# Moving weights read from two runs of 256 columns in turn, in a one-core decoder layer on Trainium2

## The chip, the cores and the metric

The kernel runs on one core of a Trainium2 chip. The metric is the device time of one execution in microseconds, lower is better. Three runs of the kernel before took 429.0, 428.86 and 430.1 us, median 429.0.

The core has five engines that matter here: TensorE (PE in the profile; its weight loads are listed apart as PEld), VectorE (DVE), ScalarE (ACT), GpSimd (POOL) and SyncE (SP), which here only issues DMA transfers. A matmul has a stationary operand, 128 columns that are loaded into the array first, and a moving operand, whose columns are then read one by one. Its result goes to a bank of PSUM, 128 partitions by 512 numbers of 32 bits.

## The reference

One layer of a decoder over 256 tokens of width 1024. Three attention mixers read one combined projection of x; their outputs go through branch projections and gates and are added. What matters for this change is what follows:

```
merged = (gates[:, :, 0] * (o_a @ w_br_a[i])
          + gates[:, :, 1] * (o_b @ w_br_b[i])
          + gates[:, :, 2] * (o_c @ w_br_c[i]))
x = layer_norm(ALPHA * x + merged @ w_out[i], ln1_g[i], ln1_b[i])
h = jnp.square(jax.nn.relu(x @ w_up[i])) @ w_down[i]
ple = jax.nn.sigmoid(x @ w_ple_gate[i]) * (p[i] @ w_ple[i])
x = layer_norm(ALPHA * x + h + ple, ln2_g[i], ln2_b[i])
```

`w_out` and `w_ple_gate` are 1024 x 1024, `w_ple` is 256 x 1024, `w_up` 1024 x 4096 and `w_down` 4096 x 1024, all in 32-bit floats.

## The kernel before

**Products in three terms.** Every operand is split into a high and a low part in the 32-bit format that PE multiplies in one pass. `prod` (L184, its matmul on L189) adds high x high, high x low and low x high into one bank of PSUM. So each product of a stationary block and a moving block is three matmuls, and each of these has its own weight load.

**The weights.** `Weights` (L80) holds a list of units. For each, SP issues one transfer of up to 128 x 1024 numbers from HBM into a ring of five buffers (`raw`, L103); ScalarE writes the high part (`whi`, L110 or L112); VectorE, for some units with GpSimd, subtracts it to make the low part (`wlo`, L119 or L123). `get` does this up to four units ahead of the use. The order of the work on each engine is written by a planner that estimates times; `pin` keeps single instructions in program order.

**Two kinds of product.** In the gates, the branch projections and the up projection the weights are the stationary operand, in blocks of 128 columns, and the activations move. There the code spreads the blocks in `whi` and `wlo` with gaps (`LOW`, L223; `UP`, L606). In the output projection, the embedding, its gate and the down projection it is the other way round: the activations are stationary, 128 tokens at a time, and the weights move, 512 columns at a time (`H` are the two halves of the 1024 columns). These blocks stand in `whi` and `wlo` without gaps.

**The stages with moving weights, in order:**

- *Output projection:* class `Wide` (L611) over the 8 blocks of 128 rows of `w_out`. For each block, two halves of the tokens (b) and two halves of the columns (c): 8 x 4 products. `go` (L623) makes one.
- *Embedding:* 2 blocks of rows of `w_ple` (`wp`, L753), 4 products each, scaled into `PL`.
- *Its gate:* `Wide` again over the 8 blocks of `w_ple_gate`; the stationary blocks are the normalised x, transposed (`x1`). The first normalisation (`ln1`) runs between.
- *Up projection:* 32 blocks, stationary weights, L891 (512 columns) and L893 (256 columns). Not of the moving kind. `relu2` and the split write the hidden activations `hT`.
- *Down projection:* `SEQ` (L819) lists the 26 blocks of its loop. Seven pairs of blocks are done by a scheme of Strassen's kind: `form` (L848) makes sums and differences of the halves of two blocks' weights, and seven products in place of eight go to seven banks (`TERMS`, `onto`, L932). Twelve single blocks go through `plain` (L944), 4 products each. Then the banks are added up, and the 6 blocks of `LATE` (L821) are added per output bank, with the second normalisation (`ln2`, L992) behind each. For the last quarter of the tokens and columns the last 512 columns are cut into two of 256 (`CUT`, L983), so that their normalisation can start earlier.

**What depends on the columns' order.** The split works column by column. `form` adds and subtracts whole halves of 512. The normalisations, the sums over banks and the output read PSUM in the natural order of columns.

**The host** (`_layout`, L1064) only reorders: it reshapes `w_out`, `w_down`, `w_ple_gate` and `w_ple` into blocks of 128 rows with all 1024 columns in their own order.

Of the kernel before, what the change touches and what calls it, by code (L numbers as in the profile page):

```python
# [19 lines left out]
D = 1024  # L20
# [123 lines left out]
def hybrid_layer(ctx: ExitStack, tc: tile.TileContext, x0, xn, pT, wqk, wva, wvb, wg, wbc, wba,  # L144
# [26 lines left out]
    ph = keep.tile([128, 2, S], F32R, name="ph")  # L171
    pl = keep.tile([128, 2, S], F32R, name="pl")
# [5 lines left out]
    t = banks.tile([128, 512], F32, name="b4", tag="b4")  # L178
# [5 lines left out]
    def prod(ps, a, b, first, last, hold=False, more=False, low=2):  # L184

        terms = [(0, 0), (0, 1)]
        terms.insert(low, (1, 0))
        for n, (x, y) in enumerate(terms):
            i = pe.matmul(ps, lhsT=a[x], rhs=b[y], start=first and n == 0, stop=last and n == 2,  # L189
                          skip_group_check=more)  # L190
            if hold and n == 0:
                pin(i)

    def gemm(ps, units, xs, k=0):

        for u in units:
            hi, lo = W.get(u)
            for o in range(0, hi.shape[1], 128):
                prod(ps, (hi[:, o:o + 128], lo[:, o:o + 128]), xs[k], k == 0, k == len(xs) - 1,
                     low=TURN["g"][k])  # L200
                k += 1
# [29 lines left out]
    for t in TASKS:  # L231
# [4 lines left out]
        elif t in "gcao":  # L236
            u, w, n = {"g": (u_g, wg, 1024), "c": (u_bc, wbc, 640), "a": (u_ba, wba, 768),
                       "o": (u_out, wout, 1024)}[t]
# [28 lines left out]
    def mmbank(shape):  # L267
        t = mm.tile([128, 512], F32, name="mm", tag="mm")
        return t[:, 0:256] if shape == 256 else t

    last = [None, None]
# [20 lines left out]
    def k_pair(a, b=None):  # L292


        k = (kp if b is None else k1).tile([128, 2, S], F32R, name="k", tag="k")
        for d, ps in ((slice(0, 128), a),) if b is None else ((slice(0, 64), a),
                                                             (slice(64, 128), b)):
            freed(act.copy(k[d, 0], ps),
                  dve.tensor_tensor(k[d, 1], ps, k[d, 0].bitcast(F32), op=ALU.subtract))  # L299
        return k  # L300
# [28 lines left out]
    def feat(f):  # L329
        ps = mmbank(256)  # L330
        gemm(ps, u_q[f], xs)
        if f > 8:
            next(side, None)
        return ps
# [133 lines left out]
    with ExitStack() as begin:  # L468
# [7 lines left out]
        with tc.high_priority(offset=1000):  # L476
# [4 lines left out]
            for k in range(KT):  # L481
                act.copy(xh[:, k], g0[:, k, 0:S])
                for a, b in cut[k]:
                    a = max(a, S)
# [3 lines left out]
        first = [next(ps_s if f < 3 else ps_t)[:, 0:S] for f in range(FIRST)]  # L488
# [8 lines left out]
    ps = feat(4)  # L497
# [35 lines left out]
    def opair():  # L533
        return wk2.tile([128, S], F32, name="o", tag="o")

    for j in range(2):
        ps = feat(5 + 4 * j)
        k = k_pair(ps)
# [6 lines left out]
        o = opair()  # L545
# [11 lines left out]
    for j in range(3):  # L557
        ps = feat(13 + 2 * j)
        k = k_pair(ps)
        q = q_pair(feat(14 + 2 * j))  # L560
        s = logits(k, q)
        o = opair()
# [12 lines left out]
    for j in range(3):  # L575
        s = logits(kA, q)
        o = opair()
# [31 lines left out]
    H = (slice(0, 512), slice(512, 1024))  # L609

    class Wide:  # L611
# [10 lines left out]

        def go(self, acc, k, b, cs, first, last, hold=False, more=False):  # L623
            hi, lo = self.ws[k]
            prod(acc, self.stat(k, b), (hi[:, cs], lo[:, cs]), k == first, k == last, hold, more)

        def step(self, k, ahead=AHEAD, bs=(0, 1), last=None, whole=None):

# [54 lines left out]
    more = p3.tile([128, 4096], F32R, name="more")  # L683
# [54 lines left out]
    def turn(b, c, ps):  # L738

        pt[b, c] = ps = ps.rearrange("p (k t) -> p k t", t=128)  # L740
        for k in range(4):
            pin(pe.transpose(ps[:, k], Y[:, b, (4 * c + k) * 128:(4 * c + k + 1) * 128], ident))  # L742
        return act.copy(x1[:, b, 4 * c:4 * c + 4, 0], ps)
# [9 lines left out]
    wp = [W.get(u, 0) for u in u_ple]  # L753
    for i in range(4):
        if i == 3:
            turn(0, 0, next(ps_a))
            low(0, 0)
        b, cs = i // 2, H[i % 2]
        t = slice(b * 128, (b + 1) * 128)
        ps = mmbank(512)  # L760
        for k in range(2):
            prod(ps, (ph[:, k, t], pl[:, k, t]), (wp[k][0][:, cs], wp[k][1][:, cs]),
                 k == 0, k == 1, True)
        act.mul(PL[:, b, cs], ps, 0.5)

# [57 lines left out]
    hT, at, room = {}, 0, 0  # L823
    for k in (*SEQ, *LATE):
        i = PAIRS.index(k) if k in PAIRS else -1
        n = 512 if i < 0 else 1792
        if i in (0, 1):
            t = p2.tile([128, 2048], F32R, name=("X", "PL")[i], tag=("X", "PL")[i])[:, 0:n]
        elif i in (2, 3) or k == 2:
            t = more[:, room:room + n]  # L830
            room += n
        else:
            t = store[:, at:at + n]
# [31 lines left out]
    for k in (*SEQ, *LATE):  # L865
        if k in PAIRS:
            i = PAIRS.index(k)
# [13 lines left out]
    for f in range(32):  # L881
# [5 lines left out]
        ps = mmbank(512).rearrange("p (b a t) -> p b a t", b=2, a=2)  # L887
        hi, lo = W.get(u_up[f][0])
        cs = [slice(k * 128, (k + 1) * 128) for k in range(KT)]
# [26 lines left out]
        h = hT[half_of[f]]  # L916
# [11 lines left out]
    P = {2: pg.acc[1][0], 3: pg.acc[1][1], 4: pg.acc[0][0], 8: pg.acc[0][1], 7: next(ps_a)}  # L928
    P.update((i, mmbank(512)) for i in (5, 1, 6))
    fresh = {1, 5, 6, 7}  # L930

    def onto(i, a, b, end=False):  # L932
        prod(P[i], a, b, i in fresh, end, more=True)
        fresh.discard(i)

    def weights(u):
# [7 lines left out]
    def plain(k, w, ids, end=False):  # L944
        for i in ids:
            b, c = {2: (1, 0), 3: (1, 1), 4: (0, 0), 8: (0, 1)}[i]
            t, cs = slice(128 * b, 128 * b + 128), H[c]
            onto(i, (hT[k][:, 0, t], hT[k][:, 1, t]), (w[0][:, cs], w[1][:, cs]), end)


    TERMS = ((2, 2, 1), (3, 6, 0)), ((7, 5, 1), (5, 3, 0)), ((1, 0, 0), (6, 4, 1)), ((4, 1, 0),)
    for k in SEQ[:-2]:
        if k not in PAIRS:
            plain(k, weights(u_dn[k][0]), (3, 2, 4, 8), k == 23)
            continue
        for u, terms in zip(u_dn[k], TERMS):
            hi, lo = weights(u)
            for i, a, c in terms:
                a = slice(128 * a, 128 * a + 128)
                onto(i, (hT[k][:, 0, a], hT[k][:, 1, a]), (hi[:, H[c]], lo[:, H[c]]),  # L960
                     k == PAIRS[-1] and i in (1, 5, 6, 7))

    def plus(o, a, b):
# [21 lines left out]
    for i, acc in enumerate(ends):  # L985
        c = slice(256 * i, 256 * i + 256)
# [30 lines left out]
    accs = (P[4], P[8]), (P[2], *ends)  # L1017
    for b in range(2):
        t = slice(128 * b, 128 * b + 128)
        for c, cs in enumerate(CUT[b]):  # L1020
            for k in LATE:
                hi, lo = ws[k]
                prod(accs[b][c], (hT[k][:, 0, t], hT[k][:, 1, t]), (hi[:, cs], lo[:, cs]), False,
                     k == 31, more=True)
            ln2(b, c, accs[b][c])


# [36 lines left out]
def _layout(x, p, w_in, w_gate, w_br_a, w_br_b, w_br_c, w_out, ln1_g, ln1_b, w_up, w_down,  # L1064
            w_ple_gate, w_ple, ln2_g, ln2_b, rel_bias):
    x = x[0]
    w_in = w_in[0]
    ar = lambda o, n: np.arange(o, o + n)
    pair = lambda base, j: ar(base + 128 * j, 128)
    iq = np.concatenate([pair(IQ, j) for j in range(4)])  # L1070
    feats = []
    feats.append(np.concatenate([ar(IK, 64), ar(AK, 64)]))
    for j in range(2):
        feats.append(pair(BK, j))
        feats += [ar(BQ + g * 256 + j * 128, 128) for g in range(3)]
    for j in range(3):
        feats += [pair(CK, j), pair(CQ, j)]
    feats += [pair(AQ, j) for j in range(3)]
    va = np.concatenate([ar(AV, 64), ar(BV, 256), ar(IW, 8)])
    vb = ar(CV, 384)  # L1080

    def moving(w, j):
        n = w.shape[1]
        kt = w.shape[0] // 128
        return w.reshape(kt // j, j, 128, n).transpose(0, 2, 1, 3).reshape(kt // j, 128, j * n)

    gate = np.concatenate([ar(b * D + f * 128, 128) for f in range(8) for b in range(3)])
    br = np.concatenate([w_br_a[0], w_br_b[0], w_br_c[0]], axis=0)
    br = _cols(br, np.arange(D))
    oh, pick = _shape_constants()  # L1090
    arrays = {
        "x0": np.concatenate([x.T.reshape(KT, 128, S), w_in[:, iq].reshape(KT, 128, 512)], axis=2),
        "xn": x.reshape(2, 128, D).transpose(1, 0, 2),
        "pT": p[0, 0].T.reshape(2, 128, S).transpose(1, 0, 2),
        "wqk": _cols(w_in, np.concatenate(feats)),
        "wva": moving(w_in[:, va], 2),
        "wvb": moving(w_in[:, vb], 2),
        "wg": _cols(w_gate[0], gate),
        "wbc": br[:, :, 384:],
        "wba": br[:, :, :384].reshape(4, 2, 128, 384).transpose(0, 2, 1, 3).reshape(4, 128, 768),  # L1100
        "wout": w_out[0].reshape(8, 128, D),
        "wup": _cols(w_up[0], np.arange(4 * D)),
        "wdn": w_down[0].reshape(32, 128, D),
        "wpg": w_ple_gate[0].reshape(8, 128, D),
        "wple": w_ple[0].reshape(2, 128, D),
        "lnrow": np.stack([ln1_g[0], ln1_b[0], ln2_g[0], ln2_b[0]]),
        "rel": rel_bias,
        "onehot": oh,
        "pick": pick,
    }  # L1110
    return {n: np.ascontiguousarray(a) for n, a in arrays.items()}
# [17 lines left out]
```

## Time and profile before

| what | value |
|---|---|
| runs, median (lowest to highest) | 429.0 us (428.86 to 430.1) |
| span of the profiled execution | 426.7 us |
| difference of the two | 2.3 us |
| TensorE, share of the span | 98% |
| TensorE's granted clock, mean | 1.00 in the stretches from 190 to 414 us |
| VectorE, ScalarE, GpSimd | 83%, 65%, 28% |
| bytes moved by DMA | 84.30 MB |
| first matmul with moving weights of the output projection | 198.8 us |
| up projection | 246 to 337 us |
| last matmul | ends at 419.8 us |

The profile is of one execution; its span runs from the first to the last instruction of the program. The runs are timed from outside, so they hold what lies around the span: 2.3 us by the median. A matmul's own duration in the profile (389 ns for 512 columns) is longer than the distance from one to the next, since matmuls follow one another in a pipeline. The distance is what a matmul costs, and it is read from rows that give a stretch and the number of matmuls in it.

### The profile page before, as it was taken

The numbers are of one execution on the slowest core, as the hardware profiler recorded it, in microseconds if no ns is written. First come the engines' busy times: TensorE is split into PE (matmuls) and PEld (weight loads), VectorE is DVE, ScalarE is ACT, GpSimd is POOL, SyncE is SP. The second block draws the span as 40 slices with busy tenths as digits, with TensorE's granted clock in tenths as the row PEclk, the third lists the DMA queues.
The fourth block names the chain that finished last, engine by engine and source line by source line (L and its number), as shares of the span: only waits on it lengthen the run. The fifth ranks groups of instructions, "written<-read, shape, count | busy, mean of one in ns | idle before, by whom it ended". The sixth has DMA issues, their size and how long they took to land.

```text
span 426.7 us, 7816 instructions
## 1 busy us (share of the span) xinstructions
PE 417.5 (98%) x2804; PEld 378.9 (89%) x2804; DVE 353.0 (83%) x646; ACT 279.3 (65%) x530; POOL 117.8 (28%) x128
## 2 busy tenths in 40 slices
PE   8999999999999999999999999999999999999993
PEld 8989999999999999999887888888888888888883
DVE  5979659898676689879967889989998798999755
ACT  6777385495888777857514667887888665567310
POOL 1659475164444556500000002232320000000001
PEclk9999999999999999999999999999999999999998
DMA  7895976567464417477851676785674287646502
GB/s 288 307 326 152 267 239 204 151 201 257 139 193 131 131 39 282 122 266 269 310 221 46 205 271 200 215 295 171 184 231 158 91 281 226 190 149 230 165 2 99
DMA packets 28301, 84.30 MB, mean 198 GB/s; under 512 B 2993, under 2 KB 7129, under 8 KB 27877
## 3 DMA queue, kind: packets, MB, share of 16 engines
q1 hardware_dynamic: 26880, 79.41, 57.3%
q10 hardware_dynamic: 1284, 4.32, 3.0%
q8 instruction: 22, 0.36, 0.4%
q14 instruction: 19, 0.15, 0.1%
q0 software_dynamic: 96, 0.06, 0.0%
HBM read 81.88 MB, written 1.90 MB: 196 GB/s over the span
## 4 chain that ended last, share of the span: by engine, by line
PE 87%; ACT 2%; DVE 2%; issue 1%; DVEq 0%; ACTq 0%
PE mm L189 37%; PE b L189 25%; PE mm L891 14%; PE mm L893 7%; PE b L347 2%; PE b L388 1%; PE b L392 1%; ACT whi L112 1%; ACT ri L517 1%; PE b L393 0%; DVE wlo L123 0%; ACT ri L513 0%; PE mm L742 0%; ACT e L419 0%; DVE X L716 0%
## 5 line engine op out<-in xcount | busy, mean ns | idle before, releaser
L112 ACT CAST whi<-raw 128x1024 fp32r<-128x1024 f32 (+3 forms) x92 | 89.9, 988 | 37.5 <-PE b L189 14.2
L123 DVE TENSOR_TENSOR wlo<-raw,whi 128x256 fp32r<-128x256 f32 (+3 forms) x118 | 98.3, 856 | 16.5 <-ACT whi L112 12.2
L189 PE MATMUL mm<-xh,whi 128*128 128x256 f32 x336 | 90.2, 280 | 0.0
L189 PE MATMUL mm<-xl,whi 128*128 128x256 f32 x336 | 88.0, 278 | 0.0
L123 POOL TENSOR_TENSOR wlo<-raw,whi 128x384 fp32r<-128x384 f32 (+1 forms) x50 | 68.1, 1370 | 71.3 <-ACT whi L112 65.6
L189 PE MATMUL mm<-xh,wlo 128*128 128x256 f32 x336 | 80.6, 281 | 0.2 <-DVE k L299 0.2
L189 PEld LDWEIGHTS mm<-xh,whi 128*128 128x128 f32 x336 | 63.1, 188 | 0.8
L891 PE MATMUL mm<-x,whi 128*128 128x512 f32 x256 | 63.4, 389 | 0.0
L189 PEld LDWEIGHTS mm<-xl,whi 128*128 128x128 f32 x336 | 63.1, 188 | 0.1
L189 PEld LDWEIGHTS mm<-xh,wlo 128*128 128x128 f32 x336 | 57.8, 188 | 0.8 <-DVE k L299 0.4
L189 PE MATMUL b<-whi,store 128*128 128x512 f32 x168 | 54.0, 389 | 0.0
L891 PEld LDWEIGHTS mm<-x,whi 128*128 128x128 f32 x256 | 45.7, 188 | 7.6
L119 DVE TENSOR_TENSOR wlo<-raw,whi 128x1024 fp32r<-128x1024 f32 (+2 forms) x38 | 43.4, 1163 | 3.9 <-ACT whi L112 3.7
L110 ACT CAST whi<-raw 128x256 fp32r<-128x256 f32 x64 | 36.8, 617 | 10.0 <-PE mm L891 5.4
L708 POOL TENSOR_TENSOR rs<-rs,half 128x1 f32<-128x1 f32 x4 | 2.7, 666 | 146.9 <-DVE rs L707 146.9
L189 PEld LDWEIGHTS b<-whi,store 128*128 128x128 f32 x168 | 31.5, 188 | 6.5
L893 PEld LDWEIGHTS mm<-x,wlo 128*128 128x128 f32 x256 | 33.8, 188 | 2.5
L893 PE MATMUL mm<-x,wlo 128*128 128x256 f32 x256 | 34.2, 276 | 0.0
L189 PE MATMUL b<-wlo,store 128*128 128x512 f32 x84 | 32.7, 389 | 0.0
L189 PE MATMUL mm<-op,whi 128*128 128x256 f32 x128 | 22.5, 280 | 0.0
L914 POOL TENSOR_TENSOR a<-a 128x128 f32<-128x128 f32 x7 | 5.3, 757 | 61.5 <-ACT a L877 55.6
L189 PE MATMUL b<-whi,x 128*128 128x512 f32 x64 | 20.5, 395 | 0.0
(223 smaller groups left out, 825.7 us busy)
## 6 DMA issues: line engine op xcount, KB each, us to landing
raw<-in_wup_dram SPq DMA_DIRECT2D x32, 512.0 KB
raw<-in_wg_dram SPq DMA_DIRECT2D x24, 512.0 KB
raw<-in_wqk_dram SPq DMA_DIRECT2D x18, 512.0 KB
raw<-in_wdn_dram SPq DMA_DIRECT2D x18, 512.0 KB
raw<-in_wout_dram SPq DMA_DIRECT2D x8, 512.0 KB
raw<-in_wpg_dram SPq DMA_DIRECT2D x8, 512.0 KB
T<-tabd SPq DMA_DIRECT2D x24, 128.0 KB
xr<-in_wdn_dram SPq DMA_DIRECT2D x6, 512.0 KB
```

Of the source, the lines that this page charges most:

```text
L110: i = nc.scalar.copy(blocks(hi, a, b), blocks(r, a, b))
L112: i = nc.scalar.copy(hi, r)
L119: i = e.tensor_tensor(lo[:, x], r[:, x], hi[:, x].bitcast(F32), op=ALU.subtract)
L123: i = e.tensor_tensor(blocks(lo, *x), blocks(r, *x), blocks(hi, *x).bitcast(F32), op=ALU.subtract)
L189: i = pe.matmul(ps, lhsT=a[x], rhs=b[y], start=first and n == 0, stop=last and n == 2, skip_group_check=more)
L347: m = pe.matmul(ss[2 * n + h][:, QC[b]], lhsT=q[d, x, c], rhs=k[d, y, 0:128 * (b + 1)], start=i == 0, stop=i == 2)
L388: pe.transpose(t[:, 128 * i:128 * i + 128], P[:, 128 * i:128 * i + 128], ident)
L392: pe.matmul(v, lhsT=V[:, 0, vh], rhs=pt[:, :, 0:256], start=True, stop=False)
L517: act.mul(r[:, h, QC[0]], r[:, h, QC[0]], iw[:, 0, n:n + 1])
L891: pe.matmul(ps, lhsT=hi[:, c], rhs=x1[:, :, k], start=k == 0, stop=False)
L893: pe.matmul(ps[:, :, 0], lhsT=lo[:, c], rhs=x1[:, :, k, 0], start=False, stop=k == KT - 1)
L914: pool.tensor_tensor(sums[2], a11, a21, op=ALU.subtract)
```

## The change

In the four places where weights move, a matmul no longer reads its 512 columns one after the other. The host stores each half of 512 columns with its even columns first (256 of them) and then its odd ones. The kernel reads the first column of the first run, the first of the second run, the second of the first, and so on. The columns reach PE in their natural order, and the results lie in PSUM as they did. Where 256 columns are read (the end of the down projection), these are two runs of 128. No instruction, transfer or tile is added or removed, and no tile is moved by the code.

```diff
+    def wide(t, cs):
+
+        h, o = cs.start // 512 * 512, cs.start % 512 // 2
+        t = t[:, h:h + 512].rearrange("p (a c) -> p c a", a=2)
+        return t[:, o:o + (cs.stop - cs.start) // 2]
+
+    def pairs(ps):
+        return ps.rearrange("p (c a) -> p c a", a=2)
...
         def go(self, acc, k, b, cs, first, last, hold=False, more=False):
             hi, lo = self.ws[k]
-            prod(acc, self.stat(k, b), (hi[:, cs], lo[:, cs]), k == first, k == last, hold, more)
+            prod(pairs(acc), self.stat(k, b), (wide(hi, cs), wide(lo, cs)), k == first, k == last,
+                 hold, more)
...
-            prod(ps, (ph[:, k, t], pl[:, k, t]), (wp[k][0][:, cs], wp[k][1][:, cs]),
+            prod(pairs(ps), (ph[:, k, t], pl[:, k, t]), (wide(wp[k][0], cs), wide(wp[k][1], cs)),
                  k == 0, k == 1, True)
...
     def onto(i, a, b, end=False):
-        prod(P[i], a, b, i in fresh, end, more=True)
+        prod(pairs(P[i]), a, b, i in fresh, end, more=True)
...
-            onto(i, (hT[k][:, 0, t], hT[k][:, 1, t]), (w[0][:, cs], w[1][:, cs]), end)
+            onto(i, (hT[k][:, 0, t], hT[k][:, 1, t]), (wide(w[0], cs), wide(w[1], cs)), end)
...
-                onto(i, (hT[k][:, 0, a], hT[k][:, 1, a]), (hi[:, H[c]], lo[:, H[c]]),
+                onto(i, (hT[k][:, 0, a], hT[k][:, 1, a]), (wide(hi, H[c]), wide(lo, H[c])),
...
-                prod(accs[b][c], (hT[k][:, 0, t], hT[k][:, 1, t]), (hi[:, cs], lo[:, cs]), False,
-                     k == 31, more=True)
+                prod(pairs(accs[b][c]), (hT[k][:, 0, t], hT[k][:, 1, t]), (wide(hi, cs), wide(lo, cs)),
+                     False, k == 31, more=True)
...
+    def turns(w):
+        return w.reshape(w.shape[0], 2, 256, 2).transpose(0, 1, 3, 2).reshape(w.shape)
...
-        "wout": w_out[0].reshape(8, 128, D),
+        "wout": turns(w_out[0]).reshape(8, 128, D),
...
-        "wdn": w_down[0].reshape(32, 128, D),
-        "wpg": w_ple_gate[0].reshape(8, 128, D),
-        "wple": w_ple[0].reshape(2, 128, D),
+        "wdn": turns(w_down[0]).reshape(32, 128, D),
+        "wpg": turns(w_ple_gate[0]).reshape(8, 128, D),
+        "wple": turns(w_ple[0]).reshape(2, 128, D),
```

## The prediction

> **What bounds the kernel now.** I read the page first, then the table of busy time by stretch, then what PE waited for, and last the chain of waits in order of time. The page:
>
> ```profile
> span 426.7 us, 7816 instructions
> PE 417.5 (98%) x2804; PEld 378.9 (89%) x2804; DVE 353.0 (83%) x646; ACT 279.3 (65%) x530; POOL 117.8 (28%) x128
> PEclk9999999999999999999999999999999999999998
> ```
>
> TensorE is busy all the time at the full granted clock, and there is a weight load for every matmul. The stretches that hold the changed matmuls (output projection from 198.8 us, embedding and its gate to 245.9, down projection from 337.0 to 419.8) read:
>
> ```profile
> core 0: us, PE busy (x) PEld busy (x) DVE busy (x) ACT busy (x) POOL busy (x), PEclk, DMA share, GB/s
> 196.00:224.00 28.00, 28.00 (x137) 23.62 (x136) 24.59 (x37) 12.82 (x19) 1.01 (x1) 1.00 0.69 249
> 335.00:405.00 70.00, 70.00 (x314) 58.12 (x313) 63.05 (x71) 41.26 (x48) 0.00 (x0) 1.00 0.63 203
> 405.00:414.00 9.00, 9.00 (x43) 7.47 (x43) 3.79 (x4) 2.08 (x3) 0.00 (x0) 1.00 0.01 2
> ```
>
> In all three PE fills the stretch. What PE waited for, in the whole run, and the largest wait of the other side:
>
> ```profile
> PE b L180 <- POOL ident masks.py:199: 1.7, 1, 1.7
> PE mm L189 <- DVE wlo L123: 0.3, 1, 0.3
> PE mm L189 <- DVE k L299: 0.2, 1, 0.2
> ACT whi L112 <- PE b L189: 18.7, 13, 5.3
> ```
>
> PE waits for nothing in the changed stages; ScalarE, which splits the weights, waits 18.7 us there for PE to give a buffer back. So the weights are ready ahead, and the end is set by how fast PE goes through its matmuls. A busy share does not tell that; the spacing does. The chain of waits (start, duration, what, how many in a row) gives it, a stretch divided by its count:
>
> ```profile
> 184.06 14.70 PE mm L189 x129
> 224.63 0.44 PE b L742 x4
> 250.61 1.36 PE mm L891 x6
> 251.97 0.91 PE mm L893 x8
> ...
> 391.85 15.41 PE b L189 x68
> 415.94 3.84 PE mm L189 x32
> ```
>
> 68 matmuls of 512 columns of the down projection take 15.41 us, 226.6 ns each. The 32 matmuls of 256 columns at the end take 120.0 each. But the 8 of L893, also 256 columns, take 113.8, and the 129 of the branch projections (256 columns too) 114.0. A third width, from the values, in the timeline of PE (start, duration of one; 15 matmuls of 384 columns stand between the first and the last, both included, at even distances):
>
> ```profile
> 83.42 0.33 PE L189 MATMUL mm<-whi,xh 128*128 128x384 f32 x1
> ...
> 85.84 0.33 PE L189 MATMUL mm<-whi,xl 128*128 128x384 f32 x1
> ```
>
> 14 steps in 2.42 us are 172.9 ns. The widths 256, 384 and 512 at 120.0, 172.9 and 226.6 lie on a line: (226.6 - 120.0) / 256 = 0.416 ns per column, and 120.0 - 256 x 0.416 = 13.4 ns that every matmul pays whatever its width. The faster 256-column rows pay 113.8 - 106.6 = 7.2. Same shape, same operation, same loads: what differs in the code is where the operands lie. The up projection's low halves are put at columns 208, 336 and so on (L606), 16 columns off the blocks of 32 in which everything lies at the end (L983 to L1025), where weights and `hT` both start at multiples of 128. So a part of the 13.4 ns, at least 6.2 of it, looks like a collision between two reads that run together: the moving columns of one matmul, and the stationary block that is loaded for the next.
>
> ```profile
> L189 PEld LDWEIGHTS b<-whi,store 128*128 128x128 f32 x168 | 31.5, 188 | 6.5
> L893 PEld LDWEIGHTS mm<-x,wlo 128*128 128x128 f32 x256 | 33.8, 188 | 2.5
> ```
>
> Each load shows 188 ns, most of a 226.6 ns matmul, so the two reads do run together. On this a sentence of its own: the Trainium skill, TensorE: Matmul & The Clock Gate, section "Step-by-step: what each phase is for", says that PE has two independent read ports on SBUF and that loading the next tile's weights takes no read bandwidth from the running matmul. By that rule there is no collision to remove and the time stays 429.0; the rows do not bear it out, since 120.0 and 113.8 stand for the same shape at the same clock, but they do not prove the collision either.
>
> **The change part by part.** *Instructions:* none is added or removed. The 561 matmuls of 512 columns on L189 (8 x 4 x 3 output projection, 2 x 4 x 3 embedding, 8 x 4 x 3 its gate, 7 x 21 + 12 x 12 in the loop of the down projection, 6 x 9 at its end) keep their operands' tiles, order and result. The largest groups of them:
>
> ```profile
> L189 PE MATMUL b<-whi,store 128*128 128x512 f32 x168 | 54.0, 389 | 0.0
> L189 PE MATMUL b<-wlo,store 128*128 128x512 f32 x84 | 32.7, 389 | 0.0
> L189 PE MATMUL b<-whi,x 128*128 128x512 f32 x64 | 20.5, 395 | 0.0
> L189 PE MATMUL b<-store 128*128 128x512 f32 x48 | 11.0, 389 | 0.0
> L189 PE MATMUL b<-wlo,x 128*128 128x512 f32 x32 | 12.6, 393 | 0.0
> ```
>
> With these go the 6 x 6 = 36 of 256 columns at the end (2 x 128 columns in turn). The up projection (L891, L893), the gates and the attention are untouched.
>
> *The host's order:* each row's halves of 512 columns are permuted inside themselves. The transfers are the same size and the same rows:
>
> ```profile
> raw<-in_wdn_dram SPq DMA_DIRECT2D x18, 512.0 KB
> raw<-in_wout_dram SPq DMA_DIRECT2D x8, 512.0 KB
> ```
>
> Cost nothing, since a permutation moves no byte count. Splits (L112, L119) and `form` (L848) work column by column on whole halves, and a half stays a half; nothing. The results in PSUM come out in natural order, so `ln1`, `ple`, the sums and `ln2` are as before; nothing. The order that the planner writes could shift if it prices the new reading differently; no row prices that. By the waits above it would have to eat ScalarE's 18.7 us of lead first, so I take 0, with 0.5 us either way in the range.
>
> *The moving read,* the only thing that has a price: instead of 512 columns one after the other, column c of the first 256, column c of the second, then c + 1 of each. The trace has no PE read of this kind, so I bound it.
>
> Lower end: the whole 13.4 ns goes, on 561 + 36 = 597 matmuls: 597 x 13.4 = 8.0 us. Half-way: what the better placed rows show, 120.0 - 113.8 = 6.2 ns less: 597 x 6.2 = 3.7 us. Upper end: a read that changes its place at every column may go at half pace. The nearest PE row is the transposes of L742, 4 x 128 columns in 0.44 us, 0.86 ns per column, about twice 0.416: 512 columns then take 440, and 561 x (440 - 226.6) + 36 x (220 - 120.0) = 119.7 + 3.6 = 123.3 us more. Another engine does read two places in turn here, and the trace has its price beside a read in a row:
>
> ```profile
> L875 DVE TENSOR_REDUCE a<-mm 128x256 f32<-128x512 f32 x23 | 15.6, 684 | 2.2 <-PE mm L893 2.2
> L397 DVE TENSOR_TENSOR ov<-b,ov 64x512 f32<-64x512 f32 x16 | 10.9, 678 | 6.3 <-ACT ov L396 6.3
> ```
>
> L875 takes its 512 columns from two places 128 columns apart in turn (`p b a t -> p b t a`) in 684 ns, L397 its 512 in a row in 678: no price for turns, though from PSUM, and at 1.3 ns per column, three times PE's. A sentence of its own on the other side: the Trainium skill, Advanced Engine Details and Errata, section "SBUF Cachelines", says that accesses which go to another 16-byte line each time are penalised and that a line needs at least two hits to hide the memory's latency; the new reading has one column per visit of a line, so by that rule the upper end would be the one. No row here shows it for PE.
>
> I take the half-way value, because it is the only smaller cost that rows of this shape show. Two runs in turn change how the moving read meets the load: it goes through each run half as fast, so the fixed march of the two reads past each other, column block by column block, is broken, and the collision is no longer the same for all blocks. Sum: span 426.7 - 3.7 = 423.0 us. The median of the runs, 429.0, is 2.3 over the span; with the same 2.3, **425.3 us**. PE stays the bound: in the stretch from 335 us it would go from 70.0 to about 68.1, and DVE's 63.05 still fits under it. By the lower end (65.9) it fits too, with 2.8 us to spare, so little or nothing is given back. After the last matmul at 419.8 us nothing moves.
>
> **The rivals.** *No change, 429.0.* The 13.4 ns belong to every pair of load and matmul, or to the load alone, and the order in which the columns are read does not touch them. For it: the same 13.4 at three widths. Against it: 113.8 for the same shape. It would give 426.7 + 2.3 = 429.0.
>
> *Half pace, slower, about 552.* PE's read path delivers less than a column per 0.416 ns when every column lies elsewhere than the last. Place: every one of the 597 matmuls. Price: 123.3 us by the transposes' 0.86 ns per column, so 429.0 + 123.3 = 552.3. It decides from the point where a column costs more than 0.416 + 13.4 / 512 = 0.442 ns, since then even a complete end of the collision does not pay for it. For it: nothing in the trace shows that PE reads scattered columns at full pace. Against it: the DVE row above.
>
> *In step with the load, slower, about 436.* Read in turn, the moving read advances through memory at half its pace and can fall in step with the load of the next stationary block, on the same side instead of the other. Then the collision does not shrink by 6.2 ns but grows, by two such steps, 12.4: 597 x 12.4 = 7.4 us, 436.4. It decides from a fixed cost above 13.4 ns per matmul. For it: the change leaves every tile where it lies, and at the end of the kernel, where both lie alike, the dearer value stands. Against it: the load's start is not tied to a column, and the reads may slide past each other.
>
> **How the numbers follow.** Forecast, fewer collisions: 0.56; its own range reaches from 420.5 (all 13.4 ns gone, and 0.5 for the planner) to 428. No change: 0.13. Half pace: 0.20. In step: 0.11. What a measurement of this kernel can tell from no change is 0.3%, 1.3 us. All but a little of the forecast lies below 427.7, so faster 0.55; same 0.14 with that little; slower 0.31 from the last two. The range runs from 420.5 to 437.5, over the forecast, no change and the reads in step; only half pace, 0.20, is left out, since nothing lies between.
>
> **What would show it.** In the chain of waits, the long row of the down projection divided by its count: about 220 ns says that the forecast's step is right, about 213 that the whole 13.4 was collision, 226.6 that it belongs to the pair, 239 the reads in step, 440 half pace. L891 must stay at 226.7 (1.36 us for 6) and L893 at 113.8, since they are untouched. The 256-column matmuls at the end should go from 120.0 to about 114. The stretch of the down projection should shorten by (7 x 21 + 12 x 12) x 6.2 = 1.8 us, with PE still waiting for nothing. The forecast is wrong if the spacing shrinks and the span does not (then DVE or a transfer has become the bound, seen as a PE wait for `wlo` on L119), or if the spacing does not shrink at all.

## The result and the profile after

The changed kernel takes 425.75 us in the median (425.53 to 426.09), the kernel before 428.93 beside it: a ratio of 0.9925, 95% interval 0.991 to 0.994, so 3.2 us less. The profiled execution has a span of 424.3 us, against 426.7. One of the five executions of `e9_up_swap`, further down, ran at a mean granted clock of 0.85 and took 467.55 us; what is said of that kernel is of the other four.

The chain of waits (start, duration, what, how many in a row; `b` and `mm` are PSUM banks by their names in the program). First the rows of the kernel before at which its stages begin:

```profile
198.76 21.78 PE b L189 x96
...
245.60 0.46 PE mm L891 x2
246.06 4.54 PE b L189 x20
...
337.20 2.06 PE b L189 x9
```

Then the changed kernel. The lines of the code are now 10 further down: L901 and L903 are the up projection's L891 and L893.

```profile
199.62 20.97 PE b L189 x96
...
236.77 7.77 PE b L189 x36
244.54 0.47 PE mm L901 x2
245.01 4.32 PE b L189 x20
...
250.72 0.92 PE mm L903 x8
251.63 1.81 PE mm L901 x8
...
335.05 0.92 PE mm L903 x8
...
408.58 5.18 PE b L189 x24
413.76 3.58 PE mm L189 x32
```

A matmul of 512 columns that reads in turn costs 215.8 ns (7.77 us for 36, 5.18 for 24) where it cost 226.6. The 256-column ones at the end cost 111.9 where they cost 120.0. The untouched up projection stays where it was, 1.81 us for 8 and 0.92 for 8. So the reading itself wins 10.8 ns per wide matmul, almost all of the 13.4 that lay over the price of the columns. But 561 x 10.8 + 36 x 8.1 = 6.4 us, and the kernel has won half of that. The stages, from the row of the first matmul of each to that of the next, in the two traces (20 of the gate's matmuls stand behind the first two of the up projection and count there):

| stage | before, us | after, us | won | matmuls alone would win |
|---|---|---|---|---|
| output projection, embedding, gate | 46.84 | 44.92 | 1.92 | 2.1 |
| up projection | 91.60 | 91.43 | 0.17 | 0.2 |
| down projection, to the last matmul | 82.58 | 81.38 | 1.20 | 4.0 |

The first two stages keep nearly all that their matmuls win. The start of the changed kernel was 0.86 us later in its profiled execution, in the stages that are the same in both; that is most of why the spans differ by 2.4 us and the medians by 3.2. The down projection kept 1.2 us of 4.0. Where the rest went stands in the table by stretch and in the waits of the changed kernel (PEld is PE's weight loads; columns: total us, times, longest us):

```profile
196.00:224.00 28.00, 28.00 (x145) 24.71 (x145) 25.25 (x39) 13.59 (x20) 1.01 (x1) 1.00 0.78 266
337.00:405.00 68.00, 66.79 (x304) 56.40 (x303) 62.01 (x69) 40.11 (x46) 0.00 (x0) 1.00 0.63 209
405.00:417.00 12.00, 12.00 (x74) 11.00 (x73) 7.42 (x12) 0.50 (x1) 0.55 (x1) 1.00 0.07 24
```

```profile
PEld b L189 <- DVE wlo L119: 2.8, 6, 1.0
PEld b L189 <- DVE b L974: 0.7, 1, 0.7
PEld mm L189 <- DVE wlo L119: 0.6, 2, 0.4
```

Before, PE waited for nothing here. Now it is idle for 1.2 us of the 68, and its weight loads wait 3.4 us for the low parts of weights. The chain that ends last no longer runs along PE in this stage:

```profile
355.33 2.36 DVE wlo L119 x2
357.71 4.15 DMA xr<-in_wdn_dram
...
361.95 1.23 DVE Y L863
...
364.23 1.22 DVE wlo L119
```

A buffer of a pair of weight blocks (`xr`) is split on VectorE, and only then the transfer for a later pair may go into it; 4.15 us later its data are there, VectorE forms the sums (L863 to L865) and splits them, and PE waits for that split.

That is the chain up to about 368 us. From there to 391 us it holds no transfer into `xr`: it runs along VectorE's sums and splits alone, and ends with a transfer into the ring `raw` (391.10 us, 5.18 us long) and the split behind it. In part of that stretch VectorE had no room before the change either. The row for ten of its microseconds, in the kernel before (columns as above):

```profile
375.00:385.00 10.00, 10.00 (x46) 8.29 (x45) 10.00 (x13) 6.29 (x7) 0.00 (x0) 1.00 0.44 130
```

VectorE (the third busy time) fills the 10.00 us, as it does after the change.

### The profile page after: what moved, and what is told of

It is laid out like the page before. It is cut to its first block, busy times and chain, and to the rows that moved or that the text cites. A ratio compares the mean times of both kernels' runs of the same rounds, so it can differ in the third digit from the quotient of the medians.

```text
span 424.3 us, 7821 instructions
## 1 busy us (share of the span) xinstructions
PE 412.9 (97%) x2804; PEld 378.2 (89%) x2804; DVE 351.7 (83%) x646; ACT 278.7 (66%) x530; POOL 119.1 (28%) x128
## 4 chain that ended last, share of the span: by engine, by line
PE 72%; DVE 10%; DMA 4%; ACT 2%; issue 2%; SPq 0%; DVEq 0%; ACTq 0%
PE mm L189 33%; PE mm L901 14%; PE b L189 13%; PE mm L903 7%; DVE wlo L119 6%; DMA xr<-in_wdn_dram 3%; PE b L356 2%; DMA raw<-in_wdn_dram 1%; PE b L397 1%; ACT whi L112 1%; DVE Y L863 1%; PE b L401 1%; DVE xr L864 1%; DVE rows L863 1%; ACT ri L526 1%
## 5 line engine op out<-in xcount | busy, mean ns | idle before, releaser
L123 DVE TENSOR_TENSOR wlo<-raw,whi 128x256 fp32r<-128x256 f32 (+3 forms) x118 | 96.8, 844 | 16.7 <-ACT whi L112 14.4
L901 PE MATMUL mm<-x,whi 128*128 128x512 f32 x256 | 63.4, 390 | 0.0
L189 PE MATMUL b<-whi,store 128*128 128x512 f32 x168 | 52.7, 381 | 0.3 <-DVE b L974 0.3
L901 PEld LDWEIGHTS mm<-x,whi 128*128 128x128 f32 x256 | 45.8, 188 | 7.5
L119 DVE TENSOR_TENSOR wlo<-raw,whi 128x1024 fp32r<-128x1024 f32 (+2 forms) x38 | 43.0, 1154 | 3.0 <-ACT whi L112 3.0
L903 PEld LDWEIGHTS mm<-x,wlo 128*128 128x128 f32 x256 | 33.8, 188 | 2.5
L903 PE MATMUL mm<-x,wlo 128*128 128x256 f32 x256 | 34.3, 277 | 0.0
L924 POOL TENSOR_TENSOR a<-a 128x128 f32<-128x128 f32 x7 | 6.3, 899 | 60.4 <-ACT a L887 48.9
```

The lines of the kernel that those rows point to most:

```text
L119: i = e.tensor_tensor(lo[:, x], r[:, x], hi[:, x].bitcast(F32), op=ALU.subtract)
L123: i = e.tensor_tensor(blocks(lo, *x), blocks(r, *x), blocks(hi, *x).bitcast(F32), op=ALU.subtract)
L901: pe.matmul(ps, lhsT=hi[:, c], rhs=x1[:, :, k], start=k == 0, stop=False)
L903: pe.matmul(ps[:, :, 0], lhsT=lo[:, c], rhs=x1[:, :, k, 0], start=False, stop=k == KT - 1)
L924: pool.tensor_tensor(sums[2], a11, a21, op=ALU.subtract)
```

## The experiments

My theory after the result: reading in turn takes 10.8 ns from every matmul of 512 columns; the first three stages keep it, and in the down projection PE is now faster than its weights come. Two questions were open: why a read in a row costs more, and what holds the weights.

### One part of the change at a time

`e1_front` reads in turn in the output projection, the embedding and its gate alone; `e2_down` in the down projection alone.

```diff
# e1_front, against the changed kernel
-        prod(pairs(P[i]), a, b, i in fresh, end, more=True)
+        prod(P[i], a, b, i in fresh, end, more=True)
...
-        "wdn": turns(w_down[0]).reshape(32, 128, D),
+        "wdn": w_down[0].reshape(32, 128, D),
# e2_down, against the changed kernel
-            prod(pairs(acc), self.stat(k, b), (wide(hi, cs), wide(lo, cs)), k == first, k == last,
+            prod(acc, self.stat(k, b), (hi[:, cs], lo[:, cs]), k == first, k == last,
...
-        "wout": turns(w_out[0]).reshape(8, 128, D),
+        "wout": w_out[0].reshape(8, 128, D),
```

> Reading in turn in the output projection, the embedding and its gate alone; the down projection reads in a row, its weights in their own order. Theory (each matmul that reads in turn costs 215.7 ns and not 226.6, and the down projection gives most of its share back because its weights come late): 216 of the 561 wide matmuls, 216 x 10.9 = 2.4 us, less about 0.4 of new waits for the weights, so 2.0 us under the kernel before, about 426.9. The down projection stays at 226.6 per matmul with no wait for weights. Rival (the gain lies in the down projection, and what the front wins is lost in the start of the up projection): under 0.5 us gained, 428.5 or more.

Measured: 426.96 us, ratio 0.9946 (0.993 to 0.9962), 2.3 us less. The front stages take 44.92 us as in the changed kernel, the down projection 82.58 as before. The theory holds.

> Reading in turn in the down projection alone. Theory: its matmuls take 215.7 ns each, 345 x 10.9 = 3.8 us less if nothing else held them, but only about 1.2 us are kept, since PE now waits for the low parts of the weights (L119); about 427.7. Rival (nothing is given back, and the rest of the expected gain was never there): 3.8 us gained, about 425.1, without waits of PE for L119.

Measured: 427.21 us, ratio 0.995 (0.9937 to 0.9963), 2.1 us less. The front stages take 46.83 us, the down projection 80.77, so here it keeps 1.8 us of 4.0, somewhat more than with the whole change (1.2) and less than half of what its matmuls win. PE waits for L119 again. The rival falls. How much is kept differs between traces of the same stage: 1.2 in the changed kernel, 1.8 here. By the ratios the two parts win 2.3 and 2.1 us, together 4.4, where the whole change wins 3.2; the intervals leave room for a part of that, and nothing run here explains the rest.

### What holds the weights in the down projection

`e3_light_after` and `e4_light_before` leave one sum of 512 columns of the three sums of a pair, which have 2048 columns together, in the changed kernel and in the one before. The lines that are not shown make the splits of the blocks themselves:

```diff
-        dve.tensor_tensor(t[:, 0:1024], r[:, 512:1536], r[:, 0:1024], op=ALU.subtract)
-        dve.tensor_tensor(r[:, 512:1024], r[:, 1024:1536], t[:, 0:512], op=ALU.subtract)
-        dve.tensor_tensor(t[:, 1024:1536], r[:, 1536:2048], r[:, 512:1024], op=ALU.subtract)
+        dve.tensor_tensor(t[:, 0:512], r[:, 512:1024], r[:, 0:512], op=ALU.subtract)
...
```

> The changed kernel with less work on VectorE in the down projection: of the sums and differences that form makes of each pair of weight blocks, one of 512 columns is left and the others are left out (the split parts are made of the unsummed blocks, so what the down projection computes is not the reference's). Per pair VectorE has 1.9 us less. Theory (in the changed kernel PE waits in the down projection because VectorE's chain of sums and splits is late): the waits go, about 3 us are gained over the changed kernel, about 422.6. Rival (the transfers of the weights are late, VectorE only passes that on): VectorE's share does not matter, and the time stays within 0.7 us of 425.7.

> The kernel before with the same sums left out on VectorE (what the down projection computes is not the reference's). Theory (before the change PE's own pace sets the end, and VectorE's chain lies under it): no change, 428.4 to 429.3. Rival (VectorE's chain held the kernel before as well): 1 us or more gained, 428 or less.

Measured: e4 429.35 us, ratio 1.0004 (0.9994 to 1.0015), no change: before, VectorE's chain lay under PE's pace. e3 424.92 us, ratio 0.9894 (0.9877 to 0.991); against the 0.9925 of the changed kernel that is 1.3 us, less than half of the 3 that I expected, and more than the rival's 0.7. The two intervals touch at 0.991, and the medians differ by 0.8 us; in the traces the down projection goes from 81.38 to 80.10 us. What is left in e3 is one long wait of PE, 1.2 us, and it stands behind a transfer:

```profile
372.71 4.37 DMA xr<-in_wdn_dram
...
377.18 0.09 DVE Y L863
...
377.79 1.23 DVE wlo L119
...
379.06 1.13 PE b L189 x4
```

`e10_no_loads` leaves the transfers out instead, for the last four of the seven pairs, and keeps all of VectorE's work:

```diff
     def load(i):
         ...
+        if i > 2:
+            return
         nc.sync.dma_start(r[:, 0], wdn[k1])
```

> The changed kernel without four of the seven pairs' transfers in the down projection: from the fourth pair on, the sums and splits are made of what the buffer xr still holds (the down projection's result is not the reference's; 4 MB less are read). VectorE, ScalarE and PE do all their work. Theory that the loop over the buffer, its transfer of about 4.2 us and VectorE's work behind it makes the low parts late: without the transfers the waits of PE on L119 fall by 2 us or more, 423.0 to 424.0. Rival (VectorE's own work per pair is the limit, since it is 62 of 68 us busy): the waits stay, 425.2 to 426.2.

Measured: 424.29 us, ratio 0.9875 (0.985 to 0.99), 2.1 us under the changed kernel by the ratios; the down projection goes from 81.38 to 79.86 us. That lies between the theory's range and the rival's. The waits do not vanish:

```profile
PEld b L189 <- DVE wlo L119: 1.5, 3, 0.9
```

So neither VectorE's work nor the transfers alone hold the stage: taking away either gives back a part, 1.3 and 2.1 us, and uncovers the other. Without the transfers VectorE is busy for all of the 20 us from 355 to 375, and a weight load of PE still waits 0.9 us for a split at 376 us. With fewer sums (e3) VectorE is busy for 6.76 us of the ten from 365 to 375, and the wait stands behind a transfer. That fits the loop in the chain above, which contains both. Three edits tried to win it back without leaving work out. `e6_six_a` and `e7_six_b` do one of the seven pairs as two single blocks:

```diff
-    SEQ = ((0, 1), 2, 3, (4, 5), 6, 7, (8, 9), 10, (11, 12), 13, (14, 15), 16, (17, 18), 19,
+    SEQ = ((0, 1), 2, 3, (4, 5), 6, 7, 8, 9, 10, (11, 12), 13, (14, 15), 16, (17, 18), 19,
# e7_six_b instead: (8, 9), 10, 11, 12, 13,
```

> The changed kernel with six pairs and not seven in the down projection: the pair of blocks 8 and 9 is done as two single blocks. PE has 3 matmuls more (24 for 21, 0.65 us), VectorE has 4.3 us less (three sums, and 1536 columns of splits). Theory (VectorE's chain of sums and splits, with the transfers that it releases, holds the down projection): more than the 0.65 is won back from the 3.2 us of waits; 0.5 to 2 us under the changed kernel, 423.7 to 425.3. Rival (the waits come from the transfers alone): no gain, 425.7 to 426.4.

> The same with the pair of blocks 11 and 12 as single blocks, and 8 and 9 a pair. Theory: as with the other pair, 0.5 to 2 us under the changed kernel; which of the two is better depends on where PE waits first, at 348 to 351 us or at 364 to 369. Rival: no gain, 425.7 to 426.4.

Measured: e6 427.07 us, ratio 0.995 (0.9937 to 0.9962); e7 426.28 us, ratio 0.9933 (0.9919 to 0.9946). Against 0.9925 the first is slower by 1.1 us, the second about the same. Less work on VectorE in total, at the price of 3 matmuls, gains nothing; my theory of this step falls. `e8_swap` splits the first block's own columns second and not third, so that its buffer comes free one split earlier:

```diff
-                (lambda i=i: wr[i][:, 1], 1024), (lambda i=i: wt[i][:, 0:1024], 1024),
-                (lambda i=i: wr[i][:, 0], 1024), (lambda i=i: last_part(i), 512))]
+                (lambda i=i: wr[i][:, 1], 1024), (lambda i=i: wr[i][:, 0], 1024),
+                (lambda i=i: wt[i][:, 0:1024], 1024), (lambda i=i: last_part(i), 512))]
...
-    TERMS = ((2, 2, 1), (3, 6, 0)), ((7, 5, 1), (5, 3, 0)), ((1, 0, 0), (6, 4, 1)), ((4, 1, 0),)
+    TERMS = ((2, 2, 1), (3, 6, 0)), ((1, 0, 0), (6, 4, 1)), ((7, 5, 1), (5, 3, 0)), ((4, 1, 0),)
```

> The changed kernel with the four parts of a pair of weight blocks in another order: the first block's own columns come second and its sums third, so the buffer xr of the pair is split, and given back for the next transfer, one VectorE split (1.2 us) earlier. Nothing else changes, and VectorE does the same work. Theory (what PE waits for in the down projection is the loop in which a buffer must be split before the transfer of the next pair but one is issued, 4.2 us before its sums): the waits shrink, by 1 us or more of the 3.2; 424.0 to 425.0. Rival (the waits come from the rate of the transfers, 209 GB/s in that stretch, which an earlier issue doesn't raise): 425.4 to 426.2.

Measured: 425.78 us, ratio 0.9929 (0.9911 to 0.9947), six runs from 424.67 to 427.36: no gain, where the theory asked for 1 us or more and the rival for none. In its trace the transfers do start earlier (that of 357.71 us, 21.7 us after the stage's first matmul, now starts 19.9 us after it), and still PE waits for splits, 1.3 us in three places. `e9_up_swap`, the same on top of the kernel e5 below, gave 421.7 us (420.15 to 422.28), ratio 0.982 (0.9801 to 0.9839), which can't be told from e5's 0.9832.

> The same order of a pair's parts on top of the up projection that reads in turn. Theory (the loop of buffer, transfer and sums): down projection shorter by 1 us or more, 420.3 to 421.2. Rival (rate of the transfers): 421.7 to 422.3 as without it.

Both results lie where the rival put them, e9 at the lower edge. The rival, the rate of the transfers, is not shown either: in the changed kernel 266 GB/s were moved from 335 to 345 us, but only 200 and 210 from 355 to 365 and from 365 to 375, where PE waits. What would make the weights come in time stays open. Shown is that PE waits for the low parts, and that VectorE's work and the transfers each hold a part of it. That the loop of split, transfer and sums sets the pace is read from the chain and not shown: the edit that shortens it by one split won nothing.

### Why a read in a row costs more

`m1_reads` and `m2_places` are kernels of their own: series of 48 matmuls on one bank each, in 32-bit operands as the layer has them (16-bit ones in bf and bt), with the other engines all but idle. Each series ran in one execution. The core of both:

```
for i in range(N):
    at = s + 128 * (i % 2)
    nc.tensor.matmul(o, lhsT=st[:, at:at + m], rhs=rhs, start=i == 0, stop=i == N - 1, ...)
```

> Not the layer but 18 series of 48 matmuls each, on data of w_down, with nothing beside them on the other engines; every series has its own tile name. What is computed is not the reference's. The spacing of a series in its steady part is what counts. Series sq: 512 columns in a row, stationary block and moving columns at the same place modulo 32 columns; sqs: the stationary block 16 columns further; tu and tus: two runs of 256 in turn, with the same two places; tug: the second run 16 columns further; qu, oc: four runs of 128 and eight of 64 in turn; tp, tf, te: two runs in turn, 2, 4 and 16 columns of each at a time; step, stepf: every second and every fourth column; sn, tn: sq and tu with a stationary block of 32 columns; hq, hqs, ht, hts: 256 columns, in a row and in turn, at both places. Theory (a collision between the moving read and the load of the next stationary block): sq 226.6, tu 215.7; hq 120, hqs 113.5, ht 112; the 11 ns shrink to a third or less with the short load (sn under 218); tu and tus may differ, since the place decides. Rival A (reading in a row costs an extra cycle every 16 columns by itself, whatever is loaded): sq and sqs 226.6 both, sn 226.6 too, te 226.6, tp and tf like tu. Rival B (one column per visit of a 16-byte line is slow): oc or stepf far over 226, at 350 and more. If the series here all show 215 in a row as well, the 226.6 come from the other engines' work and not from PE's two reads.

The chain of waits of m1; each row is one series (the first, sq, is left out, since its first matmuls take up to 792 ns each; its last 29 take 6.57 us, 226.6 ns each; pa, the first of m2, is the same case):

```profile
26.49 11.20 PE sqs L68 x48
37.69 10.36 PE tu L68 x48
48.05 10.36 PE tus L68 x48
58.41 10.36 PE tug L68 x48
68.77 13.12 PE qu L68 x48
81.89 23.43 PE oc L68 x48
105.32 15.74 PE tp L68 x48
121.06 12.02 PE tf L68 x48
133.08 11.52 PE te L68 x48
144.60 21.66 PE step L68 x48
166.26 22.08 PE stepf L68 x48
188.34 11.13 PE sn L68 x48
199.47 10.36 PE tn L68 x48
209.83 5.75 PE hq L68 x48
215.58 5.66 PE hqs L68 x48
221.23 5.36 PE ht L68 x48
```

Divided by 48: in a row 233.3 ns with the stationary block 16 columns further (sqs), and two runs of single columns in turn 215.8 in every case: both places (tu, tus), the second run 16 columns further (tug), and the short load (tn). 256 columns: 119.8 and 117.9 in a row, 111.7 in turn. So the layer's 226.6 and 120.0 come from PE alone and not from the other engines. The place matters in a row and not in turn, but not in one direction: 16 columns further is dearer by 6.7 ns at 512 columns and cheaper by 1.9 at 256, where I expected 113.5 (hqs). But the short load does not help the read in a row (sn, 231.9), though it is recorded at 110 ns and not at some 190: my expectation of under 218 falls.

> Again series of 48 matmuls and not the layer (what is computed is not the reference's). pa to ph: 512 columns in a row, the stationary block moved on by 0, 4, 8, ... 28 columns from the place of the moving ones; na, nc, ne, ng: the same at 0, 8, 16, 24 with a stationary block of 32 columns; wf, wn: blocks of 64 and 96 columns; nt, no: 384 and 128 columns in a row; bf, bt: 16-bit operands, in a row and in turn. Collision of the moving read with the load of the next block: the cost over 213.3 ns changes with the place in both sets, and falls with the width of the block (32, 64, 96, 128 columns) where the place is the same; bf, which reads half as many bytes, is at 215.7. A fixed price per matmul of reading in a row, whatever is loaded: pa to ph alike within 2 ns, wf and wn like pa. A price per column of reading in a row: nt at 0.75 of pa, and no at a quarter.

```profile
25.76 10.89 PE pb L56 x48
36.65 11.19 PE pc L56 x48
59.04 11.19 PE pe L56 x48
103.79 11.11 PE na L56 x48
114.90 11.46 PE nc L56 x48
148.55 11.05 PE wf L56 x48
159.60 11.05 PE wn L56 x48
170.66 8.35 PE nt L56 x48
179.00 5.31 PE no L56 x48
184.31 10.38 PE bf L56 x48
194.69 23.26 PE bt L56 x48
```

In a row, 512 columns cost 226.9 ns at 4 columns' distance (pb), 233.1 at 8 and 16 (pc, pe); with the load of 32 columns, 231.5 at 0 and 238.8 at 8 (na, nc). Loads of 32, 64 and 96 columns cost 231.5, 230.2 and 230.2 (na, wf, wn): no fall with the width. 384 columns cost 174.0 (nt), so it is a price per matmul and not per column. 128 columns in a row cost 110.6 (no). With 16-bit operands a read in a row is at 216.3 (bf), at the one place that was tried.

What follows: the price over the columns belongs to 32-bit reads in a row, changes with the place of the block that is loaded, and all but 2.8 ns of it goes away when two runs are read in turn. That the place counts speaks for the two reads meeting; that the load's width does not count speaks against a collision that is paid per loaded column. No series runs without loads, so the cause itself is not settled.

### The same reading in the up projection

```diff
-        ps = mmbank(512).rearrange("p (b a t) -> p b a t", b=2, a=2)
+        ps = mmbank(512).rearrange("p (a t b) -> p a t b", b=2, a=2)
...
-            pe.matmul(ps, lhsT=hi[:, c], rhs=x1[:, :, k], start=k == 0, stop=False)
+            pe.matmul(ps.rearrange("p a t b -> p (a t) b"), lhsT=hi[:, c],
+                      rhs=x1[:, :, k].rearrange("p b a t -> p (a t) b"), start=k == 0, stop=False)
...
-            pe.matmul(ps[:, :, 0], lhsT=lo[:, c], rhs=x1[:, :, k, 0], start=False,
+            pe.matmul(ps[:, 0], lhsT=lo[:, c], rhs=x1[:, :, k, 0].rearrange("p b t -> p t b"), start=False,
```

> The changed kernel, and the up projection reads in turn too: its moving activations by the two halves of the tokens in turn, the result in PSUM in that order, and the sum behind it reads it so. Theory (a matmul of 512 columns costs 215.7 ns when it reads in turn, whatever it reads, and PE sets the pace of the up projection): 256 x 11 + 256 x 1.8 = 3.3 us less in that stage, of which the down projection may give back up to 1; about 422.5 to 423.5. Rival (VectorE, 83 of 91 us busy in that stage, or ScalarE's splits take over the pace): under 1 us gained, 425 or more, with waits of PE for low parts of weights.

Measured: 421.98 us (421.61 to 422.6), ratio 0.9832 (0.9818 to 0.9847). The chain of waits of e5 shows the two kinds of matmul of the up projection:

```profile
250.76 1.73 PE mm L901 x8
252.49 0.89 PE mm L904 x8
```

216.3 and 111.3 ns, from 226.6 and 114. The stage takes 88.18 us, 3.25 less than the changed kernel's 91.43, against 3.3 expected, and nothing of it is given back: the down projection takes 80.86. This version, with e9, which can't be told from it, is the fastest of those run, 7.2 us under the kernel before and about 4 under the changed one.

## Why the prediction was right

**The time** was forecast at 425.3 and came out at 425.75, but two terms were wrong by nearly the same amount in opposite directions: the matmuls won 6.4 us and not 3.7, and about 3 of it were given back and not 0. That the sum came out so near is luck.

- *What bounds the kernel* held: PE's spacing, not its busy share, and the fixed 13.4 ns per matmul that I read from three widths. The series confirm it (174.0 at 384 columns, 119.8 at 256).
- *The gain per matmul* was mis-sized. I took 6.2 ns, half-way, since the better placed 256-column rows showed that much; it is 10.8 for 512 columns and 8.1 for 256, close to my lower end. That the place alone makes those 6.2 ns was not borne out: 16 columns further gave 1.9 (hqs), and L893, which I called the same shape, also reads its 256 columns as two pieces of 128 that lie apart. Why it costs 113.8 stays open. Reading in turn does not behave as a better place does: the place made no difference to it where it was varied (tu, tus, tug alike). The term is 6.4 us and not 3.7.
- *"Little or nothing is given back"* was wrong. I compared VectorE's 63.05 busy us with the shortened stretch and found room. The sum fits, but it is a mean over 70 us: from 375 to 385 us VectorE was busy for the whole 10.00 before the change, and elsewhere the sums of a pair wait for a transfer that waits for a buffer. About 2.8 us of the down projection's 4.0 were given back in the trace of the changed kernel, 2.2 and 2.3 in those of e2 and e5. ScalarE's 18.7 us of waiting for PE, which I read as a lead of the weights, did not measure the lead of the low parts: ScalarE still waits 16.4 us there after the change, while PE waits for L119.
- *The cause* that I named, a collision of the moving read with the next load, is supported by the place and not by the load's width. It is not shown.
- *No change* falls with the spacing, *in step with the load* too: no 32-bit series of 512 columns in two runs of single columns is above 215.8 ns.
- *Half pace* did not come for this reading but was near: four runs in turn cost 273 ns, eight 488, two columns of each run at a time 328 (qu, oc, tp). Its price was misread: the transposes of L742 take 110 ns for 128 columns, but so does a matmul of 128 columns in a row (no, 110.6), so their 0.86 ns per column shows no slow read. The DVE row that spoke against it did not show PE's behaviour, and the choice between these ends rested on little.
- *What would show it* told the terms apart: the spacing fell to 215.8 and not to 220, L901 and L903 stayed at their price, and PE, which was to wait for nothing, waited for low parts of weights on L119, which I had named as the sign that the bound had moved. The down projection became 1.2 us shorter, where its loop alone was to win 1.8.

Every second column of 32 bits cost 451 ns (step), every fourth 460 (stepf), two runs in turn 215.8. The Trainium skill, Advanced Engine Details and Errata, section "SBUF Cachelines", wants two hits on a 16-byte line. Every second column gives two hits per line and was slow, and two runs in turn, one column per visit, were fast, so here the measurement decides against the rule in both cases; for every fourth column, one hit per line, the rule and the 460 ns agree.

## What to carry to other kernels

Read the spacing of matmuls, not their share of busy time: three widths give the price of a column and the price of a matmul, and the second is what placement and order of reading can change. Where a stage is filled by PE, ask not only whether the other engines' sums fit under the shorter time: look for stretches in which one of them is already busy throughout, and for loops of buffer, transfer and split that must turn once per step. Here a faster PE waited there. A gain that one stage gives back is worth taking to a stage that has the room, as the up projection had.

## What the runs showed of the hardware that was not expected

- In 32-bit operands, 512 moving columns cost 226.9 to 234.2 ns in a row (blocks of 128 columns), depending on where the stationary block of the next matmul lies, and 215.8 when two runs of single columns are read in turn, in the three arrangements that were tried.
- More runs are dear: 273 ns for four, 488 for eight. Two runs with 2, 4 and 16 columns at a time cost 328, 250 and 240.
- Every second column costs 451 ns, twice the price, though two of the columns that are read lie in each 16 bytes.
- In 16-bit operands it is the other way round: 216.3 ns in a row, 484.6 for two runs in turn (bf, bt).
